# A hybrid recurrent block with product-key retrieval: one dense block searched from SBUF during the query, a place of its own for the first products' buffers, and staged weights in front

## The chip, the cores and the metric

The kernel runs on one core of one Trainium2 chip. The metric is the time of one execution on the device, in microseconds (us), taken several times; lower is better. The engines are TensorE (PE, with its weight loads shown as PEld), VectorE (DVE), ScalarE (ACT), GpSimd (POOL) and SyncE (SP), which here only issues transfers. Every engine works through its own queue in order.

## What is computed

One layer over 1024 tokens of width 1024, in float32. In the notation of the reference:

```python
xn = rms_norm(h, norm1_g)
p = xn @ w_in                                   # 1024 -> 1536: xa, gate, us (512 each)
ya = rg_lru_group(xa, gate, ...)                # conv of 4 taps, two sigmoid gates, a linear scan, times gelu(gate)
yb = s5_group(us, ...)                          # 32 groups, 64 complex states, chunked scan, gelu, GLU
h = h + concat[rms_norm(ya), rms_norm(yb)] @ w_out
x = rms_norm(h, norm2_g)
q = x @ wq                                      # 8 heads, two halves of 128 each
s1, s2 = q1 @ k1.T, q2 @ k2.T                   # 128 keys each
v1, i1 = top_k(s1, 16); v2, i2 = top_k(s2, 16)  # then the best 16 of the 256 sums v1 + v2
e = i1 * 128 + i2; g = softmax(best 16)         # 8 x 16 = 128 experts of 16384 per token
out = h + sum_e g * gelu(u_tab[e] . x) * v_tab[e]
result = rms_norm(out, normf_g)
```

## The kernel before, in words

**Order.** Most of the code is written as generators ("threads") that a small planner, `Merge`, interleaves: it keeps a modelled time for each engine and always continues the thread whose time plus bias is least. A thread that yields a name waits for that flag, one that yields a function waits until it is true. So the order in which instructions are traced is the planner's. A scheduler below it may move an instruction ahead on its engine where it thinks its inputs are there; `tc.keep_in_program_order(ins)` ties an instruction behind the one traced just before it on its engine. `begin` (L268) and the dense stage at the end stand under `manual_schedule`, in the order written. The planner's helper records every operation, so nearly all rows of the profile have its line, L146, and one goes by the names of tiles.

**Splits.** Matrix products run in float32r with each operand split into a high part (a ScalarE copy) and a low part (a VectorE subtraction), and three products for each pair.

**The front (`front`, L150).** `begin` loads, on SP, eight pieces of w_in (`w0`) and eight tiles of the transposed x (`xr`), and on POOL eight tiles of x (`xs`). For each of the eight it splits the weights (`wnext`, L230) and x (`split_x`), adds 24 products to eight accumulators (`held`) in PSUM, and takes some steps of the S5 set-up (`setup`, a generator on VectorE, as many steps as `PLAN` says). Then it makes four more weight pairs, tiles 8 to 11 of `wseq`, through the tag `wr` with two buffers, runs the set-up to its end, takes two squares for the first norm (`squares`, ScalarE), copies the accumulators to `Vt`, and puts the first two products of xa (`pj_product`) into PSUM. `rsqrt_x` (L210) makes the norm's factor and spreads it with products (`spr`) to `rstdb`; every projection after this is scaled by it. S5 (`quarter`), the RG-LRU (`lru_setup`, L682, and `lru`) and the remaining projections (`proj`) follow, interleaved; `wfill` keeps nine weight pairs ahead.

After that come the GLU, the two group norms (`norm`, L857) and the output product. `wo_half` (L841) loads eight tiles of w_out for a half (`wor`, two buffers), and splits each into `woh` and `wol`. `norm` makes for each of four tiles the scaled high part `ah`, the low part `al` and the square, and the sum of the squares at the end gives the factor `rg` with which the products `wop` are added to `h`. For group A these tiles are yA, in pools `fo` and `fa` that take over SBUF of the projections.

**The retrieval (`peer`, L1024).** Tokens are eight blocks of 128. Three blocks (5 to 7, "gather" blocks) fetch the chosen rows of the tables with indirect transfers on POOL (128 rows per token for u and for v, 768 row steps in all, each a transfer and one VectorE instruction). Five blocks (0 to 4, "dense" blocks) compute all experts: first products `ap` with the u table, its gelu to `aa` and to DRAM (`A_d`), then, weighted with a matrix G, products `vp` with the v table.

`query` (L1061) computes q and the scores, for the gather blocks first (`part` 0), then for the dense blocks (`part` 1): head by head, 5 blocks, each score tile copied by ScalarE to `sc` and, for dense blocks, stored to `S_d` in DRAM. During it run the top-k of the gather blocks (`topks`) and their first rows (`gathers`). `top16` (L1125) is five VectorE instructions: max of 8, index, replace, max, index.

After the query the pools `pkg` and `pq` are closed, and `ph1` (the buffers `aa` and later `hr`) and `pk2` are opened in their SBUF. `ahead` (L1500) makes the first products of 97 tiles, in half tiles; `steps` counts the halves. `choose` (L1248) searches the dense blocks one after another with `topk` (L1158), which loads the block's scores from `S_d` into `s`, runs 16 `top16` on them, and then goes on through the sums. The very first max of block 0 is pinned in program order. For block 0 each of the generator's yields waits until `steps` has reached `BEGIN + RATE * k`; later blocks are paced by `groups`. `build` (L1273) builds G with one-hot products `gp`; its group n waits for `steps >= LEAD + n` (LEAD is 23). Rows in between are limited by `allow`: 72 (`FIRST`) until step 23, then 1.6 more for each step. What is left of the rows is spread over the dense stage.

Of the kernel before, what the change touches and what calls it, by code (L numbers as in the profile page):

```python
# [149 lines left out]
def front(tc, a, cst, nd, mg):  # L150
# [79 lines left out]
    def wnext():  # L230

        parts = wseq[len(wmade)]
        if len(wmade) < 8:
            r = parts[0]
        else:
            r = pw.tile([P, 256], F32, tag="wr", name="wr", bufs=2)
            w = 256 // len(parts)
            for i, x in enumerate(parts):
                nc.sync.dma_start(r[:, w * i:w * i + w], x)
        h = pw.tile([P, 256], F32R, tag="wh", name="wh")  # L240
        lo = pw.tile([P, 256], F32R, tag="wl", name="wl")
        S.activation(h, r, AF.Copy)
        V.tensor_tensor(lo, r, h.bitcast(F32), ALU.subtract)
        wmade.append((h, lo))
# [20 lines left out]

    held = [(pu if s < 2 else pj if s < 4 else pt)("usp")[:, :256] for s in range(L)]

    def begin():  # L268
# [5 lines left out]
        for k in range(8):  # L274
# [3 lines left out]
            xrs.append(xr)  # L278
        for _ in range(WARM):
            PE.matmul(held[7][:, :P], ident, ident, start=True, stop=True)  # L280
        st, sq = setup(), squares()
        for k in range(8):
# [7 lines left out]
            xrs.append(xr)  # L290
            for _ in range(PLAN[k]):
                next(st)
            if k > 4:
                next(sq)
        for _ in range(4):
            wnext()
        for _ in st:
            pass
        for _ in range(2):
            next(sq)  # L300
# [4 lines left out]
        for i in range(2):  # L305
            pre[0, 0, i] = pp = pj("pj")
            pj_product(pp, wmade[8:12], i)
        for _ in sq:
            pass
# [372 lines left out]
    def lru_setup():  # L682
        tc.keep_in_program_order(S.dma_start(lamt, a["lru_lam"]))
        S.activation(e_, lamc, AF.Abs)
# [156 lines left out]
    def wo_half(half):  # L841

        for n in range(2):
            for k in range(4):
                if half:
                    yield "half0" if (n, k) >= (1, 2) else "cols0"
                r = po.tile([P, 512], F32, name="wor", tag="wor", bufs=2)
# [9 lines left out]
    def norm(grp, ys, dh, dl):  # L857

        gs, tot = pu("gs"), rstdb
        for k in range(4):  # L860
# [4 lines left out]
            yield  # L865
            sq = po.tile([P, T], F32, name="sq2", tag="sq2") if k else tot
# [151 lines left out]
PACE = 2.0  # L1018
WARM, PLAN = 8, (2, 6, 3, 3, 3, 3, 3, 1)
FIRST, STEP, KT, LEAD = 72, (1.6, 1.6), 2, 23  # L1020
BEGIN, RATE, FAST = 2, 0.68, 0.9


def peer(tc, a, cst, pools, h, nx, mg):  # L1024
# [36 lines left out]
    def query():  # L1061
# [13 lines left out]
        for part, (blocks, dh, dl) in enumerate(((gblocks, nx.xGh, nx.xGl), (dblocks, xDh, xDl))):  # L1075
# [6 lines left out]
            for h_ in range(8):  # L1082
# [23 lines left out]
                for n, b in enumerate(blocks):  # L1106
# [3 lines left out]
                    yield  # L1110
                    sc = pq.tile([P, 256], F32, tag="sc", name="sc", bufs=6)
# [7 lines left out]

    pkg = pools.open("pkg")  # L1120
# [28 lines left out]

    rows = pools.open("rows", "right", bufs=ROWS)  # L1150
# [6 lines left out]

    def topk(b):  # L1158
        if b >= ND:
            yield "found"  # L1160
            v, ix = found[b - ND]
        else:
# [6 lines left out]
            for h in range(8):  # L1169
                for f in range(2):  # L1170
                    top16(s[:, h, f], v[:, f, h], ix[:, f, h], b == dblocks[0] and f == 0)
# [368 lines left out]
    mg.run([(1.0, topks()), gr], until="q")  # L1540
    mg.run([], until="chosen")
    pools.close("pkg", "pq")
    ph1 = pools.open("ph1")
# [367 lines left out]
```

## Time and profile before

| | |
|---|---|
| median of 3 runs | 2580.09 us (2578.77 to 2582.99) |
| the profiled execution | 2573.88 us, its span 2572.1 us |
| busy, share of the span | PE 97%, PEld 88%, DVE 92%, ACT 52%, POOL 45% |
| instructions | 40777 |
| moved by DMA | 752.77 MB, mean 293 GB/s |

The stretches of the run, by what TensorE does in them: the front up to about 360 us, the query to about 590, first products and the building of G to about 1424, then the dense stage. In the page's 40 slices VectorE is at eight tenths or more in most slices, with dips around 270 to 350, near 1250 to 1420 and at the start.

In a row of a timeline stand start and length in us, engine, line, operation, output and inputs, shapes, and in brackets the idle time of the engine just before, with what ended it. In a row of stretches stand the stretch and its length, then busy time (and instructions) of PE, PEld, DVE, ACT and POOL, the granted clock of TensorE, the DMA share and GB/s. In the chain of waits stand start, length and what the run waited for.

### The profile page before, as it was taken

Reading aid. Unit: us, or ns where it says so; the run is one execution under the profiler, and the core shown is the slowest. Engines: PE = TensorE matmul, PEld = TensorE weight load, DVE = VectorE, ACT = ScalarE, POOL = GpSimd, SP = SyncE. Lnnn points to the kernel's source line nnn. Section 1 sums busy time; section 2 is a strip of 40 time slices with the busy share of each in tenths; the row PEclk is TensorE's granted clock in tenths of the full one; section 3 lists DMA queues with packets and bytes.
Section 4 is the critical chain, followed back from the end, with each engine's and each line's share of the span. In section 5 each row is a group of like instructions: output and inputs, shape, how many; then the busy total and the mean of one; then the engine's idle time right before and its main releaser. Section 6 shows DMA issues by size and latency. Waiting matters only on the chain.

```text
span 2572.1 us, 40777 instructions
## 1 busy us (share of the span) xinstructions
PE 2486.4 (97%) x14639; PEld 2252.0 (88%) x14639; DVE 2363.1 (92%) x4545; ACT 1332.5 (52%) x2389; POOL 1152.1 (45%) x803
## 2 busy tenths in 40 slices
PE   8998999999989999999999999999999999999997
PEld 7776889999989999999999988888888888888886
DVE  7998669997999999999977699999999999999998
ACT  5567434332468777877877444333344344333442
POOL 1000000353456466675554465555556556555551
PEclk9999999999999999999999999999999999999999
DMA  5113124687899999999999999999999999999994
GB/s 186 31 43 111 65 90 139 209 279 270 280 351 353 338 326 333 351 333 335 356 367 350 359 384 357 353 353 356 354 348 370 355 356 351 352 359 353 350 350 152
DMA packets 302201, 752.77 MB, mean 293 GB/s; under 512 B 29744, under 2 KB 128240, under 8 KB 297264
## 3 DMA queue, kind: packets, MB, share of 16 engines
q0 software_dynamic: 112896, 411.09, 43.9%
q1 hardware_dynamic: 186576, 336.28, 36.8%
q10 hardware_dynamic: 2528, 2.80, 0.3%
q8 instruction: 115, 1.88, 0.3%
q14 instruction: 86, 0.70, 0.1%
HBM read 662.92 MB, written 85.98 MB: 291 GB/s over the span
## 4 chain that ended last, share of the span: by engine, by line
PE 62%; DVE 27%; DMA 4%; issue 4%; ACT 2%; POOL 1%; SPq 0%; DVEq 0%; ACTq 0%; POOLq 0%
PE vp L146 26%; PE ap L146 17%; PE total L146 7%; DVE row L146 4%; PE qp L146 4%; DVE hb L146 3%; PE wop L146 3%; PE gp L146 2%; DVE ul L146 2%; DVE oh L146 2%; DVE ohA L146 2%; DVE ix L146 2%; DVE v L146 1%; PE pj L146 1%; DVE ohB L146 1%
## 5 line engine op out<-in xcount | busy, mean ns | idle before, releaser
L1339 POOL DMA_INDIRECT row<-in_peer_u_dram,idx x384 | 562.5, 1465 | 697.5 <-DVE act L146 268.3
L1339 POOL DMA_INDIRECT row<-in_peer_v_dram,idx x384 | 576.7, 1502 | 439.1 <-DVE hb L146 273.3
L146 PE MATMUL ap<-xDl,uh 128*128 128x320 f32 x2048 | 645.5, 315 | 9.0 <-ACT aa L146 8.2
L146 PE MATMUL ap<-xDh,ul 128*128 128x320 f32 x2048 | 635.6, 310 | 5.4 <-DVE ul L146 5.2
L146 PE MATMUL ap<-xDh,uh 128*128 128x320 f32 x2048 | 634.9, 310 | 0.0
L146 DVE SCALAR_TENSOR_TENSOR hb<-row,act,hb 128x1024 f32<-128x1024 f32 x384 | 494.0, 1286 | 6.7 <-DMA row<-in_peer_v_dram,idx 1.8
L146 DVE CUSTOM_DVE_ANT_0 row<-row,xg 128x1024 f32<-128x1024 f32 x384 | 458.7, 1219 | 3.0 <-DMA row<-in_peer_u_dram,idx 2.6
L146 PE MATMUL vp<-vl,hh 128*128 128x512 f32 x1024 | 398.7, 389 | 0.0
L146 PE MATMUL vp<-vh,hl 128*128 128x512 f32 x1024 | 398.5, 389 | 0.0
L146 PE MATMUL vp<-vh,hh 128*128 128x512 f32 x1024 | 398.5, 389 | 0.0
L146 PEld LDWEIGHTS ap<-xDl,uh 128*128 128x128 f32 x2048 | 386.1, 189 | 12.0 <-ACT aa L146 9.5
L146 PEld LDWEIGHTS ap<-xDh,ul 128*128 128x128 f32 x2048 | 386.2, 189 | 8.3 <-DVE ul L146 7.0
L146 PEld LDWEIGHTS ap<-xDh,uh 128*128 128x128 f32 x2048 | 385.7, 188 | 0.0
L146 ACT ACTIVATE gq<-gt 128x640 f32<-128x640 f32 x128 | 174.4, 1363 | 319.2 <-DVE hr L146 242.1
L146 PEld LDWEIGHTS vp<-vh,hh 128*128 128x128 f32 x1024 | 192.2, 188 | 40.2
L146 PEld LDWEIGHTS vp<-vl,hh 128*128 128x128 f32 x1024 | 192.2, 188 | 39.5 <-issue 0.4
L146 PEld LDWEIGHTS vp<-vh,hl 128*128 128x128 f32 x1024 | 192.2, 188 | 38.8
L146 ACT ACTIVATE ohB<-ohB,kt 128x128 f32<-128x128 f32 x480 | 202.2, 485 | 0.0
L146 PE MATMUL gp<-ohB,ohA 128*128 128x128 f32 x1280 | 172.1, 277 | 18.7 <-DVE ohB L146 14.8
L146 ACT ACTIVATE aa<-ap 128x320 f32<-128x320 f32 x194 | 84.1, 435 | 199.0 <-PE ap L146 183.2
L146 PEld LDWEIGHTS gp<-ohB,ohA 128*128 128x128 f32 x1280 | 158.9, 191 | 27.8 <-issue 11.5
L146 DVE TENSOR_TENSOR ul<-ur,uh 128x1024 fp32r<-128x1024 f32 x128 | 156.1, 1220 | 20.0 <-ACT uh L146 20.0
(450 smaller groups left out, 4457.6 us busy)
## 6 DMA issues: line engine op xcount, KB each, us to landing
ur<-in_uT_dram SPq DMA_DIRECT2D x128, 512.0 KB
vr<-in_peer_v_dram SPq DMA_DIRECT2D x128, 512.0 KB
gt<-G_d SPq DMA_DIRECT2D x32, 1280.0 KB
G_d<-gs SPq DMA_DIRECT2D x79, 512.0 KB
A_d<-aa SPq DMA_DIRECT2D x96, 320.0 KB
hr<-A_d SPq DMA_DIRECT2D x96, 320.0 KB
wqr<-in_wq_dram SPq DMA_DIRECT2D x31, 512.0 KB
row<-in_peer_u_dram,idx POOLq DMA_INDIRECT x384
```

The costliest lines, as they stand in the source:

```text
L146: return fn(*args, **kw)
L1339: G.indirect_dma_start(out=r, out_offset=None, in_=a["peer_v" if at >= P else "peer_u"], in_offset=bass.IndirectOffsetOnAxis(ap=idx[n][:, ...
```

## The change

In front, weight tiles 8 to 11 get places of their own (`wp`, in the pool `fx`), are loaded on SP right behind the transposed x, and are split inside the last of the eight steps, ahead of that step's set-up and square. The rest of the set-up and of the squares moves behind the first two products of xa, one square after each set-up step. The high parts of tiles 12 to 19 and the first instruction of `lru_setup` are pinned in program order. In `wo_half`, five of the eight tiles of half 0 (`OWN`) come through three buffers `wor0` in `fa` instead of `wor`. `norm` for group A makes all four high and low parts first, then the squares.

In the retrieval, ScalarE copies the scores of dense block 0 into one SBUF tile `s0` (8 heads x 2 x 128) and they are neither stored nor loaded again. A thread `search0` with bias 0.0 runs beside the query from the flag `split` on, which `query` sets when it has issued the last weight split: for each head whose copy has been traced (`seen`) it runs the two `top16`, the first max of each pinned. `topk` of block 0 takes these results, so 17 yields are left of it; `BEGIN` and `RATE` become 1 and 1.0. `ph1` is opened on the right side, before the pool of the rows, instead of on the left after `pkg` and `pq` are closed.

```diff
@@ wnext
         if len(wmade) < 8:
             r = parts[0]
+        elif len(wmade) < 12:
+            r = wp[:, len(wmade) - 8]
         else:
             r = pw.tile([P, 256], F32, tag="wr", name="wr", bufs=2)
...
-        S.activation(h, r, AF.Copy)
+        ins = S.activation(h, r, AF.Copy)
+        if 12 <= len(wmade) < 20:
+            tc.keep_in_program_order(ins)
         V.tensor_tensor(lo, r, h.bitcast(F32), ALU.subtract)
...
+    wp = px.tile([P, 4, 256], F32, name="wp")
@@ begin
+        for n in range(4):
+            for i, x in enumerate(wseq[8 + n]):
+                nc.sync.dma_start(wp[:, n, P * i:P * i + P], x)
         for _ in range(WARM):
             PE.matmul(held[7][:, :P], ident, ident, start=True, stop=True)
...
             xrs.append(xr)
+            if k == 7:
+                for _ in range(4):
+                    wnext()
             for _ in range(PLAN[k]):
                 next(st)
             if k > 4:
                 next(sq)
-        for _ in range(4):
-            wnext()
-        for _ in st:
-            pass
-        for _ in range(2):
-            next(sq)
         Vt[0] = pvt.tile([P, 16, L, 16], F32, name="Vt", tag="Vt", bufs=2)
...
             pj_product(pp, wmade[8:12], i)
+        for _ in st:
+            next(sq, None)
         for _ in sq:
             pass
@@ lru_setup
-        S.activation(e_, lamc, AF.Abs)
+        tc.keep_in_program_order(S.activation(e_, lamc, AF.Abs))
@@ wo_half
-                r = po.tile([P, 512], F32, name="wor", tag="wor", bufs=2)
+                own = half == 0 and (n, k) in OWN
+                r = pa_.tile([P, 512], F32, name="wor0", tag="wor0", bufs=3) if own else \
+                    po.tile([P, 512], F32, name="wor", tag="wor", bufs=2)
@@ norm
-        for k in range(4):
+
+        def parts(k):
             g_ = cols[:, k, 7 + grp:8 + grp]
             S.activation(dh[:, k], ys[k], AF.Copy, scale=g_)
             yield
             V.scalar_tensor_tensor(dl[:, k], ys[k], g_, dh[:, k].bitcast(F32), ALU.mult, ALU.subtract)
             yield
+        if grp == 0:
+            for k in range(4):
+                yield from parts(k)
+        for k in range(4):
+            if grp:
+                yield from parts(k)
             sq = po.tile([P, T], F32, name="sq2", tag="sq2") if k else tot
@@ constants
+OWN = ((0, 0), (0, 2), (1, 0), (1, 1), (1, 3))
-BEGIN, RATE, FAST = 2, 0.68, 0.9
+BEGIN, RATE, FAST = 1, 1.0, 0.9
@@ query
+                    if part and n == 0:
+                        if h_ == 0:
+                            s0.append(pk.tile([P, 8, 2, P], F32, name="s", tag="s", bufs=1))
+                        S.activation(s0[0][:, h_], p_[:, :256].rearrange("p (f k) -> p f k", f=2), AF.Copy)
+                        seen[0] += 1
+                        yield
+                        continue
                     sc = pq.tile([P, 256], F32, tag="sc", name="sc", bufs=6)
@@ peer
+    s0, seen = [], [0]
...
+    ph1 = pools.open("ph1", "right")
     rows = pools.open("rows", "right", bufs=ROWS)
...
+    def search0():
+        yield "split"
+        v = pk.tile([P, 2, 8, 16], F32, name="v", tag="v")
+        ix = pk.tile([P, 2, 8, 16], U32, name="ix", tag="ix")
+        for h in range(8):
+            yield lambda: seen[0] > h
+            for f in range(2):
+                top16(s0[0][:, h, f], v[:, f, h], ix[:, f, h], f == 0)
+        s0.append((v, ix))
+        mg.flag("s0")
+        yield
...
+        elif b == dblocks[0]:
+            v, ix = s0.pop()
         else:
             s = pk.tile([P, 8, 2, P], F32, name="s", tag="s", bufs=1)
...
-                    top16(s[:, h, f], v[:, f, h], ix[:, f, h], b == dblocks[0] and f == 0)
+                    top16(s[:, h, f], v[:, f, h], ix[:, f, h])
...
-    mg.run([(1.0, topks()), gr], until="q")
+    mg.run([(1.0, topks()), (0.0, search0()), gr], until="q")
     mg.run([], until="chosen")
+    mg.run([], until="s0")
     pools.close("pkg", "pq")
-    ph1 = pools.open("ph1")
     pk2 = pools.open("pk2", bufs=2)
```

## The prediction

> **What bounds the kernel now.** I read the page first, then the stretches, and only then the instructions on either side of each hole in TensorE's work.
>
> ```profile
> PE 2486.4 (97%) x14639; PEld 2252.0 (88%) x14639; DVE 2363.1 (92%) x4545; ACT 1332.5 (52%) x2389; POOL 1152.1 (45%) x803
> ```
>
> ```profile
> 30.00:60.00 30.00, 20.54 (x115) 16.44 (x115) 21.29 (x83) 17.19 (x39) 3.43 (x12) 0.83 0.16 45
> 150.00:200.00 50.00, 46.95 (x274) 36.17 (x273) 49.69 (x81) 33.83 (x45) 0.00 (x0) 0.97 0.18 42
> 590.00:600.00 10.00, 8.78 (x61) 8.33 (x59) 0.00 (x0) 1.56 (x5) 2.14 (x3) 1.00 0.97 354
> 700.00:720.00 20.00, 17.38 (x120) 16.79 (x120) 20.00 (x72) 11.09 (x27) 10.87 (x9) 1.00 0.93 320
> 720.00:740.00 20.00, 16.29 (x107) 14.67 (x106) 20.00 (x66) 10.42 (x27) 9.87 (x8) 1.00 0.93 307
> 740.00:760.00 20.00, 17.40 (x119) 16.43 (x120) 20.00 (x63) 13.51 (x36) 12.01 (x9) 1.00 1.03 408
> 850.00:900.00 50.00, 47.36 (x335) 46.01 (x335) 50.00 (x172) 34.38 (x85) 22.83 (x16) 1.00 0.94 334
> 1000.00:1050.00 50.00, 45.37 (x323) 44.32 (x323) 50.00 (x167) 33.65 (x84) 21.62 (x16) 1.00 0.94 335
> 1600.00:1800.00 200.00, 200.00 (x985) 172.80 (x984) 194.67 (x179) 78.08 (x86) 107.33 (x80) 1.00 0.96 355
> ```
>
> The columns after the length are busy time of PE, PEld, DVE, ACT and POOL, then clock, DMA share and GB/s. TensorE sets the time: the dense stage (1600 to 1800) has no hole. So an edit pays only where it closes a hole, or where the engine ahead of a hole is freed. All holes together are 2572.1 - 2486.4 = 85.7 us. In the front (150 to 200) VectorE is fuller than TensorE, so time that only TensorE wins there does not all reach the end. From 700 to 760 TensorE misses 2.62 + 3.71 + 2.60 = 8.9 us with VectorE at 100%.
>
> **Edit 1, own weight places (the w_in tiles 8 to 11).** TensorE, then ScalarE, then VectorE, around the first hole:
>
> ```profile
> 29.91 1.12 PE L146 MATMUL usp<-wh,xl 128*128 128x256 f32 x8
> 40.49 0.80 PE L146 MATMUL pj<-xl,wh 128*128 128x512 f32 x1 [9.46 <-ACT Vt L146]
> 41.08 0.63 PE L146 MATMUL pj<-xh,wl 128*128 128x512 f32 x1
> 41.51 0.63 PE L146 MATMUL pj<-xh,wh 128*128 128x512 f32 x1
> ...
> 44.66 0.39 PE L146 MATMUL pj<-xh,wh 128*128 128x512 f32 x1
> 44.88 0.39 PE L146 MATMUL pj<-xl,wh 128*128 128x512 f32 x1
> ```
>
> ```profile
> 30.73 0.42 ACT L146 ACTIVATE wh<-wr 128x256 fp32r<-128x256 f32 x1 [2.03 <-DMA wr<-in_w_in_dram]
> ...
> 40.07 2.27 ACT L146 ACTIVATE Vt<-usp 128x256 f32<-128x256 f32 x8
> ```
>
> ```profile
> 37.05 0.42 DVE L146 TENSOR_TENSOR wl<-wr,wh 128x256 fp32r<-128x256 f32 x1 [2.69 <-ACT wh L146]
> 38.12 0.42 DVE L146 TENSOR_TENSOR wl<-wr,wh 128x256 fp32r<-128x256 f32 x1 [0.64 <-ACT wh L146]
> ...
> 45.48 1.00 DVE L146 TENSOR_SCALAR sq<-rc 128x8 f32<-128x8 f32 x1 [4.28 <-ACT xs L146]
> ```
>
> The held products end at 31.03. The third weight tile has to wait for a buffer, is split on ScalarE just ahead of the wl at 37.05, and the accumulators' copies (Vt) stand behind it on ScalarE, so TensorE starts 9.46 us late. With places of their own the four tiles are all issued right behind the last xT transfer on SP: eight issues of 64 KB each, with nothing behind them on SP that is needed sooner. The second tile landed at 30.7 when two were asked for; I take 32 for the fourth. Then come its split (0.42), one Square (about 1.2, like the 128x1024 ah at 255.04 below, 1.13) and the first Vt copy, so TensorE restarts near 33.9 (32 + 0.42 + 1.2 + 0.3): 6.6 us sooner. VectorE's holes are 2.69 + 0.64 + 4.28 = 7.6 us; it will still wait about 3 us for the same tiles, but the eight Vt copies then end near 36 and the five squares left near 42, 3.5 us ahead of 45.48, so it wins about 4.5. The pins on the later splits, and on the Abs of the RG-LRU setup, only keep them behind the square root and the broadcast; the products that need those weights wait for that broadcast anyway, and if that cover failed four splits of 0.42 would show. Both engines are nearly full later in the front, so the term lies between the two: **-5.5** (ends -3, if only part of VectorE's hole goes, and -8, if tiles land by 30).
>
> A hole also costs clock. Products start 0.43 us apart after the hole (41.08, 41.51) and 0.22 apart later (44.66, 44.88). A shorter hole shows up too:
>
> ```profile
> 78.12 2.08 PE L146 MATMUL gt<-xc,wab 128*128 128x512 f32 x2 [2.28 <-ACT r__1031 L146]
> ```
>
> ```profile
> 78.00:80.00 2.00, 1.88 (x3) 0.85 (x4) 1.90 (x4) 0.37 (x2) 0.00 (x0) 0.50 0.00 0
> ```
>
> After 2.28 us of idling the clock was 0.50, so my remaining hole of 2.9 us keeps its slow start and I book no clock gain in this term. The Trainium skill ("TensorE: Matmul & The Clock Gate", Part 1) has the clock fall only after an idle window of about 3.4 us; by that the slow start would go too, an estimate of 1.7 us more if it costs what it does at the seam below. The row at 78 us disagrees, and it decides.
>
> **Edit 2, staged w_out tiles and the order in norm.**
>
> ```profile
> 252.30 0.63 ACT L146 ACTIVATE woh<-wor 128x512 fp32r<-128x512 f32 x1 [2.79 <-DMA wor<-in_w_out_dram]
> 254.51 0.63 ACT L146 ACTIVATE woh<-wor 128x512 fp32r<-128x512 f32 x1 [1.58 <-DMA wor<-in_w_out_dram]
> 255.04 1.13 ACT L146 ACTIVATE ah<-yA,cols 128x1024 fp32r<-128x1024 f32 x1
> ```
>
> ```profile
> 256.23 0.80 PE L146 MATMUL wop<-wol,ah 128*128 128x512 f32 x1 [4.33 <-ACT ah L146]
> ```
>
> ```profile
> 256.23 5.92 PE wop L146 x13
> ```
>
> Two buffers make the third and fourth tile late, and the third scaled input (ah) stands behind them on ScalarE. With five places all four tiles of the first column half are asked for at once, and all ah and al are made ahead of the squares. The hole is 4.33. The chain of waits (second fence) has the 13 products after it at 5.92 us, where 13 at the spacing of 0.22 take 2.9, so 3.0 more are lost to the clock. The squares move back by at most three ah of 1.13, but are no longer behind 4.4 us of waiting, so the norm that releases the PSUM tiles is not later. I keep 2.3 of the 7.3 for transfers that share the DMA engines with the loads of x: **-5** (ends 0, if ScalarE then waits for the first four instead, and -7.3).
>
> **Edit 3, the seam after the query.** ScalarE, TensorE and VectorE there, and TensorE's clock:
>
> ```profile
> 601.68 1.28 ACT L146 ACT_TABLE_LOAD   x1 [9.10 <-DMA S_d<-sc]
> ```
>
> ```profile
> 603.46 0.53 PE L146 MATMUL ap<-xDl,uh 128*128 128x320 f32 x1 [4.68 <-ACT aa L146]
> ```
>
> ```profile
> 603.79 0.49 DVE L146 MAX8 v<-s 128x8 f32<-128x128 f32 x2 [15.56 <-DMA s<-S_d]
> ...
> 605.88 1.21 DVE L146 CUSTOM_DVE_ANT_0 row<-row,xg 128x1024 f32<-128x1024 f32 x1
> ```
>
> ```profile
> 603.00:605.00 2.00, 1.54 (x6) 1.54 (x7) 1.21 (x9) 1.68 (x3) 0.00 (x0) 0.65 0.21 83
> 605.00:607.00 2.00, 2.00 (x10) 2.00 (x9) 2.00 (x8) 0.00 (x0) 0.00 (x0) 0.50 0.21 81
> ```
>
> The first product buffer (aa) lies where score tiles lay whose stores were still out, so ScalarE waited 9.10 us and TensorE 4.68; the clock then lost 2 x 0.35 + 2 x 0.50 = 1.7. With ph1 at a place of its own on the right side both go: **-6.4** (ends -5, where the 1.28 us table load shows, and -6.4). Eight stores of 128 KB and one load of 1 MB leave SP's queue; its work lies beside, so that is 0. The eight copies to s0 take the place of eight of the same size: 0.
>
> VectorE sat 15.56 us in front of the pinned first search. 603.79 to 605.88 holds one head short of one index, so a head costs about 2.3 us, eight heads 18. When they run is set by the flag that `search0` waits for, set once the last q weights are split:
>
> ```profile
> 574.72 1.22 DVE L146 TENSOR_TENSOR wql<-wqr,wqh 128x1024 fp32r<-128x1024 f32 x1
> ```
>
> So no split of the query is behind them: seven heads fill 576 to 592, the eighth follows its scores. What they push back is some nine gather rows of 1.21 us, which fit into the 15.56 that VectorE regains. The searches are pinned; behind them on VectorE stand rows and the splits of the second u tiles, not needed for a while. **0** (ends 0, and +3, if one split comes a head's search late).
>
> After the seam VectorE has 18 us less to do and starts 15 us sooner, and BEGIN and RATE spread block 0's remaining 17 steps up to step 18, ahead of the build at 23. The 8.9 us missing from 700 to 760 should fall to what later blocks lose at the same point (50 - 47.36 = 2.6 and 50 - 45.37 = 4.6, mean 3.6). That is -5.3; I take **-4** since block 1's search now cannot start early (ends 0 and -12, if the next block's start gains too).
>
> **Sum.** -5.5 - 5 - 6.4 + 0 - 4 = -20.9 us. The profiled execution took 2573.88 (span 2572.1 and 1.8 around it), so 2553.0; the median of the runs, 2580.09, lies 6.2 above the profiled one, so about **2559.2**. All good ends give -33.7, all bad ends -5.
>
> **Rivals.** *Only the seam counts.* VectorE stays the pace of the front and the staged tiles only move the wait: -3, 0, -6.4, +1 and 0 make -8.4, 2571.7 of the median. For it: 49.69 of 50 at 150 to 200. Against it: VectorE's own holes at 37 to 45 go as well. *The edits do not do what they say in time:* the holes close, but from 600 to 1250 VectorE, full in every row above, returns them as later waits for ohB and ul; only about -3 is left, 2577. Against it: it has 18 us less to do there. *The other side: pinned splits parked on ScalarE.* The eight pinned high parts (tiles 12 to 19) still go through two buffers, and where one is not there, all of ScalarE waits, with S5 and the RG-LRU behind it, instead of passing it by.
>
> ```profile
> 36.61 0.42 ACT L146 ACTIVATE wh<-wr 128x256 fp32r<-128x256 f32 x1 [5.46 <-DMA wr<-in_w_in_dram]
> ```
>
> At this row's 5.46 a tile, less what the first two tiles save since they can be loaded far ahead, six waits make 32.8 us against -20.9: +11.9, 2592. It decides from 20.9 / 6 = 3.5 us a tile. Against it: by the time of the pins VectorE, which frees the buffers, is no longer held up by its own hole of 4.28.
>
> **How the numbers follow.** The forecast 0.62, only the seam 0.22, nothing left 0.10, parked splits 0.06. A measurement of this kernel tells about 0.2%, 5.2 us, from no change: the first two are faster, with some of the second's lower part falling within; the third is no change. So faster 0.83, same 0.11, slower 0.06. The likeliest case alone spans 2549 to 2569. Down to 2546 takes in half of the good ends, up to 2577 the second rival and part of the third, and about 2 in 10 is left out.
>
> **What would show it.** Right: the hole ahead of the first pj product under 4 us and its start near 33.9; no wait for wor between two ah; the first aa without a wait for S_d, and no 15 us on a MAX8; PE over 18.5 of 20 in the three stretches after the build's start. Wrong: ScalarE waits for wr between 40 and 80 us that are longer than before; a TensorE wait for ul right after the seam; a hole at the first wop product that only changes its releaser to the squares or the norm; or a first ap product after the seam (603.46) that comes less than 10 us sooner although the holes ahead of it are gone.

## The result, and the profile after

The changed kernel took 2556.0 us (median of 6 runs, 2552.3 to 2556.9), the kernel before, measured beside it, 2579.5 us (2578.0 to 2583.0). The ratio is 0.9908 with a 95% interval of 0.9895 to 0.9922. Measured a second time (below) it was 0.9921, 0.9894 to 0.9947. The forecast was 2559.2 us, the range 2546 to 2577. The profiled execution took 2555.21 us with a span of 2553.3 us, against 2573.88 and 2572.1 before: 18.7 us less in the profiles, 23.5 us less in the medians. Where the other 5 us are is one of the questions below.

From the page of the changed kernel, the busy time of the engines over the span:

```profile
PE 2482.5 (97%) x14639; PEld 2252.1 (88%) x14639; DVE 2364.9 (93%) x4545; ACT 1337.2 (52%) x2389; POOL 1157.9 (45%) x803
```

TensorE's busy time fell by 3.9 us only, its holes from 85.7 to 2553.3 - 2482.5 = 70.8 us. The stretches of the changed kernel that answer to those shown of before (length, busy time of PE, PEld, DVE, ACT and POOL, clock, DMA share, GB/s):

```profile
30.00:60.00 30.00, 26.13 (x168) 20.59 (x168) 27.93 (x96) 19.43 (x43) 3.41 (x12) 0.94 0.11 29
150.00:200.00 50.00, 45.53 (x275) 35.33 (x273) 49.82 (x79) 33.43 (x44) 0.00 (x0) 1.00 0.18 41
590.00:600.00 10.00, 10.00 (x70) 10.00 (x69) 10.00 (x36) 2.16 (x5) 7.71 (x6) 1.00 0.95 361
700.00:720.00 20.00, 19.93 (x144) 19.50 (x143) 20.00 (x41) 14.86 (x37) 16.95 (x11) 1.00 1.03 370
720.00:740.00 20.00, 18.28 (x127) 17.36 (x127) 18.44 (x45) 13.89 (x34) 16.05 (x13) 1.00 1.04 409
740.00:760.00 20.00, 18.77 (x135) 18.35 (x134) 18.88 (x59) 14.42 (x32) 9.39 (x8) 1.00 1.04 408
850.00:900.00 50.00, 48.11 (x344) 47.17 (x344) 50.00 (x146) 39.77 (x93) 25.78 (x17) 1.00 0.95 337
```

Against before, VectorE does 6.6 us more between 30 and 60 us (27.93 for 21.29), the seam (590 to 600) has no hole and a full VectorE, and from 700 to 760 us TensorE misses 3.0 us where it missed 8.9.

The first pj product in the changed kernel, on TensorE:

```profile
33.46 0.51 PE L146 MATMUL pj<-xl,wh 128*128 128x512 f32 x1 [2.29 <-ACT Vt L146]
33.80 0.60 PE L146 MATMUL pj<-xh,wl 128*128 128x512 f32 x1
34.19 0.63 PE L146 MATMUL pj<-xh,wh 128*128 128x512 f32 x1
```

The hole of 9.46 us is 2.29 us, and the start, 33.46, is 7.0 us sooner. In this execution the products behind it still start 0.34 to 0.43 us apart.

ScalarE and then TensorE ahead of the gs products:

```profile
244.36 1.14 ACT L146 ACTIVATE ah<-yA,cols 128x1024 fp32r<-128x1024 f32 x1
245.40 0.62 ACT L146 ACTIVATE woh<-wor 128x512 fp32r<-128x512 f32 x1
245.92 1.14 ACT L146 ACTIVATE ah<-yA,cols 128x1024 fp32r<-128x1024 f32 x1
247.11 0.63 ACT L146 ACTIVATE woh<-wor 128x512 fp32r<-128x512 f32 x1
247.65 0.67 ACT L146 ACTIVATE sg<-glp,cols 128x512 f32<-128x512 f32 x1
248.22 1.15 ACT L146 ACTIVATE ah<-yA,cols 128x1024 fp32r<-128x1024 f32 x1
```

```profile
248.62 0.39 PE L146 MATMUL wop<-wol,ah 128*128 128x512 f32 x1
...
260.01 1.95 PE L146 MATMUL gs<-ones,rstdb 128*128 128x1 f32 x16 [1.14 <-DVE rstdb L146]
```

No ah waits for a wor tile, and the hole of 4.33 us behind the first wop products is gone. What is left is 1.14 us ahead of gs.

ScalarE at the seam:

```profile
585.91 0.39 ACT L146 ACTIVATE sc<-sp 128x256 f32<-128x256 f32 x1 [0.35 <-PE sp L146]
586.32 1.28 ACT L146 ACT_TABLE_LOAD   x1
589.10 0.44 ACT L146 ACTIVATE aa<-ap 128x320 f32<-128x320 f32 x1 [1.50 <-PE ap L146]
```

The table load follows the last score copy without the wait of 9.10 us, and the first aa copy waits for its own product.

To see where time is won, the start times of six events cut each trace into stages (us, each a difference of two start times in the trace). "Front" ends with the first wop product; the others with the first gs product, the first ap product, the third copy of aa, the 49th copy of aa, and the first vp product. All rows but the last two are single profiled executions; the two kernels with added products (below) are not in the table.

| kernel | front | to gs | to first ap | to 3rd aa | to 49th aa | to first vp |
|---|---|---|---|---|---|---|
| before | 250.2 | 16.1 | 323.6 | 19.0 | 202.7 | 664.3 |
| before, again | 255.0 | 14.5 | 323.1 | 19.1 | 204.0 | 665.5 |
| before, third | 254.4 | 14.6 | 323.6 | 18.6 | 203.7 | 675.4 |
| changed | 248.6 | 11.4 | 323.7 | 12.5 | 196.9 | 663.5 |
| changed, again | 247.9 | 11.3 | 326.0 | 12.5 | 198.0 | 661.5 |
| front undone | 254.6 | 11.8 | 325.7 | 12.5 | 197.4 | 662.5 |
| staged tiles undone | 248.5 | 15.8 | 323.9 | 12.5 | 200.1 | 667.0 |
| ph1's place undone | 250.9 | 11.2 | 328.4 | 12.8 | 196.8 | 661.0 |
| pace undone | 249.1 | 11.1 | 323.3 | 12.5 | 199.7 | 663.1 |
| search behind the query, pace undone | 250.5 | 11.5 | 323.8 | 17.5 | 204.4 | 663.6 |
| search released after the query | 252.0 | 11.2 | 323.8 | 16.4 | 197.8 | 663.4 |
| pins undone | 248.4 | 11.2 | 323.3 | 12.5 | 196.0 | 661.6 |
| median with the stage as before | 254.5 | 15.2 | 323.6 | 19.0 | 203.7 | 665.5 |
| median with the stage as changed | 249.1 | 11.3 | 323.9 | 12.5 | 197.4 | 662.5 |

The last two rows take, for each stage, the runs in which that stage's edit is undone or done: for the front the three of before and "front undone" against all others but "pins undone"; to gs the three of before and "staged tiles undone" against the rest; the other stages the three of before against the runs of the changed kernel that keep the search in the query ("pins undone" among them), "ph1's place undone" left out at the 3rd aa. The differences are -5.4, -3.9, +0.3, -6.5, -6.3 and -3.0, together -24.8; the medians of the runs differ by 23.5 and, measured a second time, by 22.1. So the 18.7 us between the two first profiles are the exception, and most of it lies in the front: its -1.5 there is -5.4 between medians. The last stage of the third profile of before is 10 us longer than the others', which is not explained.

### The profile page after: what moved, and what is told of

Its sections match the earlier page's. It is cut to its first block, busy times and chain, and to the rows that moved or that the text cites. A ratio compares the mean times of both kernels' runs of the same rounds, so it can differ in the third digit from the quotient of the medians.

```text
span 2553.3 us, 40753 instructions
## 1 busy us (share of the span) xinstructions
PE 2482.5 (97%) x14639; PEld 2252.1 (88%) x14639; DVE 2364.9 (93%) x4545; ACT 1337.2 (52%) x2389; POOL 1157.9 (45%) x803
## 3 DMA queue, kind: packets, MB, share of 16 engines
q0 software_dynamic: 112896, 411.09, 43.9%
## 4 chain that ended last, share of the span: by engine, by line
PE 60%; DVE 28%; issue 5%; DMA 4%; ACT 2%; POOL 1%; DVEq 0%; SPq 0%; POOLq 0%; ACTq 0%
PE vp L146 26%; PE ap L146 17%; PE total L146 6%; DVE hb L146 5%; DVE row L146 3%; PE wop L146 3%; PE qp L146 3%; DVE ul L146 2%; PE gp L146 2%; DVE oh L146 2%; DVE ohA L146 2%; DMA ur<-in_uT_dram 1%; DVE ix L146 1%; DVE ci L146 1%; DVE v L146 1%
## 5 line engine op out<-in xcount | busy, mean ns | idle before, releaser
L1379 POOL DMA_INDIRECT row<-in_peer_u_dram,idx x384 | 581.5, 1514 | 664.7 <-DVE scv L146 242.1
L1379 POOL DMA_INDIRECT row<-in_peer_v_dram,idx x384 | 563.4, 1467 | 448.8 <-DVE hb L146 262.7
L146 DVE TENSOR_TENSOR h<-h,vp 128x1024 f32<-128x1024 f32 x128 | 155.6, 1216 | 19.6 <-PE vp L146 18.2
```

The lines of the kernel that those rows point to most:

```text
L146: return fn(*args, **kw)
L1379: G.indirect_dma_start(out=r, out_offset=None, in_=a["peer_v" if at >= P else "peer_u"], in_offset=bass.IndirectOffsetOnAxis(ap=idx[n][:, ...
```

## The experiments

**The front undone.** The four own weight places, their early splits, the pins and the new order of set-up and squares go; everything else stays.

```diff
-        elif len(wmade) < 12:
-            r = wp[:, len(wmade) - 8]
...
-        ins = S.activation(h, r, AF.Copy)
-        if 12 <= len(wmade) < 20:
-            tc.keep_in_program_order(ins)
+        S.activation(h, r, AF.Copy)
```

> Edit 1 undone (no own weight places, no pins on ScalarE), the rest as in the changed kernel. Theory, from the two traces: the first pj product goes back from 33.5 to 40.5 us, but VectorE and a slow clock near 82 to 88 us had taken nearly all of that back, so that by 186 us only 1.4 us are lost, and so the whole takes about 1.4 us more than the changed kernel: about 2557.5 us against 2556. Rival, the term as predicted: 5.5 us are lost by 186 us and at the end, about 2561.5 us.

Measured: 2562.1 us beside 2582.5 for before, ratio 0.9922 (0.9905 to 0.9938). The front took 254.6 us, 5.9 more than in the profiled change and 4.4 more than in the profile of before, though up to the first wop product its TensorE program is that of before. The run times cannot tell 1.4 from 5.5 us. That holds for the four kernels measured together here (the front, the staged tiles, ph1's place and the pace undone): their ratios of 0.9922 to 0.9933 lie inside the 0.9894 to 0.9947 that the unedited change showed the second time, so what each edit is worth is read from single traces. In the trace the loss is 5.9 us at the first wop product and 8 to 9 us from the first ap product on. So the theory was built on a profile of before that was not typical (next experiment), and the rival, the predicted 5.5, holds.

**The kernel before, twice more.** Nothing edited.

> The kernel before once more, nothing edited, for a second profile of it. Theory: its stretch of clock 0.50 behind the held sums stays (a hole of 9.5 us), the one near 78 us comes at another time or a second one follows near 87 us, and the first wop product lies up to 4.4 us behind the 250.15 us of its first profile. Rival: the stretch belongs to the program, 250.15 within 0.5 us.

> As the run before it: a third profile of the unchanged kernel before. Theory: the first wop product between 250 and 255 us, with the clock's stretch near 80 or near 90 us, and later as the stretch covers more of the 40 products that stand there without a hole. Rival: 250.15 us within 0.5 us.

Measured: first wop products at 254.96 and 254.41 us. Stretches of the first profile of before:

```profile
78.00:82.00 4.00, 3.88 (x8) 2.07 (x8) 3.79 (x7) 2.14 (x5) 0.00 (x0) 0.58 0.00 0
86.00:97.00 11.00, 10.78 (x93) 9.75 (x94) 11.00 (x17) 6.93 (x11) 0.00 (x0) 1.00 0.18 50
```

and of the second:

```profile
78.00:82.00 4.00, 2.70 (x8) 1.20 (x8) 3.79 (x7) 3.09 (x6) 0.00 (x0) 1.00 0.00 0
86.00:97.00 11.00, 10.77 (x55) 8.77 (x56) 10.41 (x17) 4.72 (x9) 0.00 (x0) 0.54 0.17 50
```

The same program has its slow clock once at 78 to 82 us, where TensorE has few products, and once at 86 to 97 us, where it works almost without a hole: 93 matmuls were done in those 11 us in the first execution and 55 in the second. Three of four executions of this front had the late one. The profile on which the prediction stood was the exception, 4.3 us short of the median of 254.5. The theory held.

These two profiles differ from the first at the seam as well. TensorE and ScalarE in the second:

```profile
596.63 1.22 PE L146 MATMUL sp<-kT,qt 128*128 128x128 f32 x4 [3.64 <-issue]
```

```profile
604.68 1.28 ACT L146 ACT_TABLE_LOAD   x1 [3.74 <-PE ap L146]
```

The two waits from which Edit 3 was made up, 9.10 us of ScalarE for the stores and 4.68 us of TensorE for aa, stand in neither. The table load waits for TensorE's own products (3.74 us here, 4.11 in the third profile), and TensorE loses its time among the last scores (3.64 + 0.27 us here, 1.90 + 1.39 in the third). The stage is as long all the same: 19.1 and 18.6 us against 19.0.

**The changed kernel again.**

> The changed kernel once more, nothing edited. Theory: where the clock of 0.50 falls between 70 and 96 us differs from one execution to the next of the same program (78 to 82 us in the profiled run of before, 86 to 97 us in the run with edit 1 undone, whose program is that of before up to there), so that the first wop product (248.6 us in the profiled run of the change) moves by up to 3 us with no edit at all. Rival: the stretch belongs to the program, and the first wop product comes within 0.5 us of 248.6.

Measured: 2556.7 us beside 2578.8, ratio 0.9921 (0.9894 to 0.9947). Stretches of the first profile of the change, then of this one:

```profile
72.00:80.00 8.00, 4.79 (x16) 2.26 (x16) 7.83 (x14) 5.91 (x9) 0.00 (x0) 1.00 0.09 26
82.00:90.00 8.00, 7.97 (x46) 6.38 (x47) 7.73 (x12) 3.50 (x6) 0.00 (x0) 0.60 0.24 68
```

```profile
72.00:80.00 8.00, 6.90 (x20) 3.31 (x18) 7.83 (x14) 6.00 (x9) 0.00 (x0) 0.57 0.11 33
82.00:90.00 8.00, 8.00 (x48) 6.64 (x47) 8.00 (x12) 3.38 (x6) 0.00 (x0) 0.57 0.19 51
```

The clock differs at 72 to 80 us, with the same program. Behind the hole of 2.29 us at 33 us it was 0.50 for some 3.5 us in the first profile and 1.00 here (0.94 and 1.00 as the mean of 30 to 60 us). The first wop product moved by only 0.7 us, but over the seven profiles that share this front it lies between 247.9 and 252.0. The theory held.

**Products that keep TensorE busy.** 26 products with a zero matrix, which add nothing to the sum, in the holes of 77 to 82 us; then 36 more, most of them at 31 and 70 us.

```diff
                     us_product(o, s + e, k, w)
+                    if s + e == 0 and k in (3, 4):
+                        for _ in range(6 if k == 3 else 20):
+                            nc.tensor.matmul(o, zero, w[k][1], start=False, stop=False)
```

> The changed kernel with 26 added products of 128x256 with a zero matrix, which add zero to the first usp sum, laid into TensorE's short holes between 77 and 82 us. Theory: they keep TensorE's clock at 1.00 through 82 to 90 us, the 41 products there take 4.3 us instead of 6.7, and the first wop product comes 2 us or more sooner than in the unedited change of the same call. Rival: VectorE is the pace there, the clock or not, and the first wop product comes within 0.5 us of it or later.

> As the kernel before it, with 18 more such products behind the held sums (31 to 33 us) and 16 more in the hole of 2.3 us at 70 to 72 us. Theory: the first pj products also start at 0.22 us instead of 0.43 us apart, 1.5 to 2 us more are won by 40 us, and no stretch of clock 0.50 is left between 30 and 100 us; the first wop product comes 3 to 5 us sooner than in the unedited change. Rival: VectorE and ScalarE set the time of the next holes, so that it wins no more than the kernel before it.

Measured: 2555.8 us (ratio 0.9908, 0.9883 to 0.9932) and 2562.4 us (0.9940, 0.9918 to 0.9961), with 2556.7 for the unedited change beside them. In the first of them:

```profile
82.00:90.00 8.00, 8.00 (x72) 7.02 (x71) 8.00 (x14) 5.10 (x8) 0.00 (x0) 1.00 0.25 68
```

```profile
247.97 0.39 PE L146 MATMUL wop<-wol,ah 128*128 128x512 f32 x1
```

The clock held at 1.00 through 82 to 90 us, and 72 matmuls were done there instead of 46 to 48, some ten of them the added ones. But the first wop product came as in the unedited kernel (247.94). So the rival has the number; its reason, that VectorE is the pace with the clock or without it, the trace does not bear out. Two rows of VectorE lie ahead of and behind the stretch, the first two `Wr<-inr,Ec` after 60 us. In the change again, then with the 26 products:

```profile
69.62 0.68 DVE L146 TENSOR_TENSOR Wr<-inr,Ec 128x508 f32<-128x508 f32 x1
113.70 0.69 DVE L146 TENSOR_TENSOR Wr<-inr,Ec 128x508 f32<-128x508 f32 x1 [2.56 <-PE inr L146]
```

```profile
71.19 0.68 DVE L146 TENSOR_TENSOR Wr<-inr,Ec 128x508 f32<-128x508 f32 x1
112.61 0.69 DVE L146 TENSOR_TENSOR Wr<-inr,Ec 128x508 f32<-128x508 f32 x1 [1.88 <-PE inr L146]
```

At the second row VectorE waits for TensorE. In each of the two fronts the time between the two rows grows as the mean clock falls:

| kernel | mean clock, 82 to 98 us | first row | second row | between |
|---|---|---|---|---|
| before | 1.00 | 76.21 | 115.70 | 39.5 |
| before, again | 0.68 | 76.71 | 120.64 | 43.9 |
| before, third | 0.68 | 76.19 | 120.18 | 44.0 |
| front undone | 0.68 | 76.47 | 120.31 | 43.8 |
| 26 products added | 1.00 | 71.19 | 112.61 | 41.4 |
| changed | 0.80 | 70.56 | 114.34 | 43.8 |
| changed, again | 0.79 | 69.62 | 113.70 | 44.1 |
| ph1's place undone | 0.68 | 71.12 | 116.55 | 45.4 |
| search released after the query | 0.59 | 70.70 | 117.38 | 46.7 |

The other three profiles with the new front and its pins fit in (0.79, 0.79 and 0.68 with 44.0, 44.1 and 45.6 us). From the second row to the first wop product it is 134.2 to 134.6 us in all of these, and 135.4 with the 26 products. So the held clock was worth some 2.5 us at the second row. About 1 us of that went later: at 148 us ScalarE waits 5.10 us for a w_in load, where it waits 4.14 in the change again. The rest is hidden, since this execution was 0.6 to 1.6 us late at the first row already, after a slower clock between 34 and 42 us (0.65, against 0.80 and 1.00 in the two profiles of the change). That the first wop products agree is thus a coincidence of one profile; the run times are too coarse for 1.5 us. With the further products the clock is 1.00 as well, but the planner put a gt product 5.3 us later, the time between the rows was 43.3 us, and the front took 251.9 us; whether a better place for them would win something was not tried.

**The pins alone undone**, those on the eight weight splits; the one on Abs stays.

```diff
-        ins = S.activation(h, r, AF.Copy)
-        if 12 <= len(wmade) < 20:
-            tc.keep_in_program_order(ins)
+        S.activation(h, r, AF.Copy)
```

> Only the pins of the eight weight splits (tiles 12 to 19) on ScalarE undone; own weight places, staged tiles, seam and search as in the changed kernel. Theory: the pins cost and save nothing; the first wop product lies between 247.9 and 250.9 us as in the profiles of the change, about 2556 us. Rival: the pins keep VectorE's wl late (ScalarE waits for wr of 1.55, 1.02 and 1.23 us between 80 and 86 us); without them these waits go and the first wop product comes 2 us or more sooner than 247.9.

Measured: 2559.3 us (2551.7 to 2565.9) beside 2581.0, ratio 0.9919 (0.9897 to 0.9941). TensorE's first pj product, and the stretch of it:

```profile
38.19 0.80 PE L146 MATMUL pj<-xl,wh 128*128 128x512 f32 x1 [6.58 <-ACT Vt L146]
```

```profile
30.00:60.00 30.00, 23.23 (x145) 19.33 (x143) 27.72 (x110) 19.30 (x43) 3.84 (x12) 0.89 0.15 44
```

Without the pins four more splits and the RG-LRU's first steps stand ahead of the Vt copies, and TensorE restarts 4.7 us later than in the change. Yet the first wop product came at 248.4. VectorE did 27.72 us of work between 30 and 60 us here, as in the change (27.93), and 21.48 us in the kernel with the front undone. So, as far as one profile can show it, what counts is that the own places close VectorE's holes, and TensorE's restart carries little: the first `Wr<-inr,Ec` row came at 71.92 us here, against 69.62 to 71.12 in the seven profiles with pins.

**The staged tiles undone.**

```diff
-                own = half == 0 and (n, k) in OWN
+                own = False
...
-            for k in range(4):
-                yield from parts(k)
         for k in range(4):
-            if grp:
-                yield from parts(k)
+            yield from parts(k)
```

> Edit 2 undone (w_out through two buffers, the scaled inputs and squares in the old order), the rest as in the changed kernel. Theory: TensorE's hole of about 4.3 us ahead of the first wop product comes back, the gs product comes 4.8 us later than in the changed kernel, and the loss stays to the end: about 2561 us. Rival: the front and the search make up for it later, less than 2 us more at 583 us (the first ap product) and at the end: 2556 to 2558 us.

Measured: 2563.3 us beside 2582.5, ratio 0.9929 (0.9903 to 0.9956). TensorE has the hole again:

```profile
254.68 0.80 PE L146 MATMUL wop<-wol,ah 128*128 128x512 f32 x1 [4.41 <-ACT ah L146]
```

The gs products came 4.4 us later than in the change and the first ap product 4.6 us later: the loss stays, as the theory had it.

**The place of the first products' buffers undone.** ph1 is opened on the left again, behind the closing of the score tiles; the search stays in the query.

```diff
-    ph1 = pools.open("ph1", "right")
...
     pools.close("pkg", "pq")
+    ph1 = pools.open("ph1")
```

> Only the place of the first products' buffers undone: they are again opened where the score tiles lay, while block 0's scores are still searched from SBUF. Theory: the wait of about 9 us on ScalarE and of 4 to 5 us on TensorE at the seam (about 590 to 600 us) comes back, the clock is slow for some 4 us behind it, and 6.5 us are lost at the third product; the 9 us gained after the seam, from VectorE, stay: about 2562.5 us at the end. Rival: VectorE uses the hole for rows and index work and gives 3 us or more of it back by 760 us, so that only 0 to 3.5 us more are left at the end.

Measured: 2561.5 us beside 2582.5, ratio 0.9926 (0.9909 to 0.9944). ScalarE at its seam, and two stretches:

```profile
597.68 1.28 ACT L146 ACT_TABLE_LOAD   x1 [4.57 <-DMA S_d<-sc]
598.97 0.89 ACT L146 ACTIVATE aa<-ap 128x320 f32<-128x320 f32 x2
```

```profile
570.00:590.00 20.00, 20.00 (x142) 19.66 (x140) 20.00 (x108) 4.62 (x12) 5.69 (x6) 1.00 0.66 223
590.00:600.00 10.00, 9.93 (x70) 9.45 (x69) 10.00 (x44) 4.51 (x10) 4.61 (x4) 1.00 0.79 225
```

ScalarE waits 4.57 us for the stores, half of before, and TensorE misses 0.07 us. From the first ap product to the third aa copy it took 12.8 us, 0.3 more than in the change and 6.2 less than before. The theory fell: with the search in the query, the place closes next to nothing. Between the first gs and the first ap product it lost 4.5 us against the median; its loads of u and wq stand in another order on SP there. But the clock's mean was also 0.96 in each of 400 to 440, 480 to 520 and 520 to 560 us, where the first profile of the change has 1.00; the change again has 0.96 in the last two of them and lost 2.3 us in this stage with nothing edited. So these 4.5 us cannot be put down to the edit.

**The search put back behind the query**, with its scores read back and the old pace; the buffers keep their own place.

```diff
-                    if part and n == 0:
...
-        elif b == dblocks[0]:
-            v, ix = s0.pop()
...
-BEGIN, RATE, FAST = 1, 1.0, 0.9
+BEGIN, RATE, FAST = 2, 0.68, 0.9
...
-    mg.run([(1.0, topks()), (0.0, search0()), gr], until="q")
+    mg.run([(1.0, topks()), gr], until="q")
```

> Block 0's search put back behind the query, from scores read back into SBUF, with the old pace constants; the first products' buffers stay at their own place. Theory: the seam stays closed on TensorE (first ap product near 583.7, the third aa copy near 596), VectorE waits for the scores again and has 18 us more to do after it, and the 9 to 10 us gained between 690 and 760 us go: aa copies 48 to 180 come 9 us later than in the changed kernel, about 2565 us in all. Rival: VectorE was not the cause of that gain, the leads change by 3 us or less, about 2557 to 2559 us.

Measured: 2574.6 us beside 2578.8, ratio 0.9979 (0.9965 to 0.9993): most of the gain is gone. TensorE and VectorE at the seam:

```profile
586.42 0.71 PE L146 MATMUL sp<-kT,qt 128*128 128x128 f32 x4 [0.24 <-issue]
587.90 0.71 PE L146 MATMUL sp<-kT,qt 128*128 128x128 f32 x4 [0.77 <-issue]
...
590.75 0.71 PE L146 MATMUL sp<-kT,qt 128*128 128x128 f32 x4 [1.98 <-ACT sc L146]
```

```profile
599.95 0.49 DVE L146 MAX8 v<-s 128x8 f32<-128x128 f32 x2 [15.49 <-DMA s<-S_d]
```

```profile
570.00:590.00 20.00, 17.75 (x122) 16.81 (x120) 11.52 (x19) 4.04 (x11) 15.32 (x13) 1.00 0.96 342
590.00:600.00 10.00, 9.25 (x53) 9.25 (x54) 0.05 (x1) 2.99 (x6) 0.00 (x0) 0.83 0.79 308
```

The own place did not keep the seam closed: TensorE loses 3.0 us on the last scores, as it does in the second and third profile of before, then the clock is 0.83, and the stage takes 17.5 us. After the seam 7.5 us more go (204.4 against 196.9). In all the first vp product came 14.8 us later than in the change, 1.9 of them from the front, and the medians differ by 17.9, where the theory had 9.

**The search released after the query**, its scores still in SBUF, without store or load.

```diff
     def search0():
-        yield "split"
+        yield "q"
```

> Block 0's scores still stay in SBUF (no store, no load of them), but their search is released only when the whole query is done, not during it. Theory: the seam stays closed on TensorE, because one of five score stores of each head is gone and the first buffers have their own place (third aa copy within 1 us of the first ap product's lead, near 596 to 598); VectorE no longer waits 15 us, but its 18 us of search fall behind the seam, and 5 to 8 us of the gain between 690 and 800 us go: about 2562 us. Rival: what counts is only that the scores need not be read back; then all but 2 us of the gain stays, 2556 to 2558 us.

Measured: 2563.1 us beside 2581.0, ratio 0.9924 (0.9902 to 0.9946). TensorE, and the stretches:

```profile
588.72 0.71 PE L146 MATMUL sp<-kT,qt 128*128 128x128 f32 x4 [1.34 <-issue]
590.20 1.22 PE L146 MATMUL sp<-kT,qt 128*128 128x128 f32 x4 [0.77 <-issue]
...
611.31 0.63 PE L146 MATMUL ap<-xDh,ul 128*128 128x320 f32 x1 [3.55 <-DVE ul L146]
```

```profile
570.00:590.00 20.00, 18.10 (x126) 17.33 (x125) 16.48 (x63) 5.13 (x13) 16.64 (x12) 1.00 0.88 295
590.00:600.00 10.00, 9.80 (x58) 9.80 (x59) 10.00 (x59) 3.20 (x7) 1.08 (x3) 0.83 0.74 252
```

On VectorE the search runs from 582 to 604 us here, where it runs from 564 to 589 in the change: the last score copy starts at 592.63, so some 11 us of it lie behind the query. VectorE's wait of 15 us is gone, one of five stores is gone, the place is own, and still the stage to the third aa takes 16.4 us. Then ul comes 3.55 us late, behind the search and the steps that follow it. The lag behind the change grows from 7.2 us at the third aa copy to 14.5 at the fifth, and 6.5 us of it are won back before the 49th, so that the stage after the seam is as in the change (197.8). Both the theory (seam closed) and its rival (2 us) fell.

What goes with the seam is in the row of 570 to 590 us. In the change it reads:

```profile
570.00:590.00 20.00, 20.00 (x141) 19.79 (x140) 20.00 (x110) 5.77 (x12) 3.75 (x4) 1.00 0.56 173
```

With the search there, VectorE is full of it and takes few gathered rows: POOL is busy for 3.75 us and the DMA share is 0.56 (5.69 and 0.66 with ph1's place undone). Without it POOL has 15 to 17 us of gathers and the share is 0.96 and 0.88. Over all profiles of this study, nine have a share of 0.56 to 0.75 there and take 12.5 to 12.8 us to the third aa; five (before three times, and the two above) have 0.88 to 0.96 and take 16.4 to 19.1, whatever the place of the buffers. That the stores come out late because they share the DMA engines with gathers fits all of these. But ahead of the last scores the traces name only "issue" or ScalarE's own copy, not the stores, and no run slowed the gathers alone; so it is argued, not shown.

**The pace alone undone**, BEGIN and RATE as before.

```diff
-BEGIN, RATE, FAST = 1, 1.0, 0.9
+BEGIN, RATE, FAST = 2, 0.68, 0.9
```

> Only the two pace constants undone (BEGIN 2 and RATE 0.68 instead of 1 and 1.0). Theory: the 9 us gained between 690 and 760 us come from VectorE having 18 us less to do after the seam, whatever the pace; the lead at 760 us changes by 2 us or less and the whole stays within 2 us of the changed kernel's 2556. Rival: the spreading of block 0's steps closes the holes; with the old pace the missing busy time of 8.9 us in 700 to 760 comes back, about 2565 us.

Measured: 2563.1 us (2557.0 to 2567.5) beside 2582.5, ratio 0.9933 (0.9916 to 0.9950). In the profile the stage after the seam is 199.7 us, 2.3 above the median of the change and within its spread of 196.0 to 200.1. The rival's 9 us are excluded by the trace. Whether the pace is worth 0 or 2 us is not settled, and the time of the runs would allow more.

No kernel of these beats the changed one by more than its measurement can tell.

## Why the prediction was right, and where not

**Edit 1, -5.5.** Measured -5.4 between the medians of four and seven profiles, front against front, and 5.9 with the edit undone. The restart was forecast at 33.9 and came at 33.46. The gain is there early: at the first `Wr<-inr,Ec` row it is 5.8 us between the medians, and 5.7 between the two first profiles. Two parts of the reasoning did not hold. "The term lies between the two" engines: the run without pins speaks for VectorE's share alone. And the pins do not "only keep them behind the square root": they hold the hole at 2.29 us instead of 6.58, at no price at the end. The clock's stretch at 82 to 97 us was not in the sum at all, since the one profile at hand showed it elsewhere. It costs both fronts: they mostly take 44 us from the first row to the second, where 39.5 and 41.4 were enough at a clock of 1.00. That it drops out of the difference was luck, for the prediction does not weigh it.

"I book no clock gain" was right in the first profile and wrong in the second, where the clock stayed at 1.00 behind the same hole and VectorE's first row came 0.9 us sooner. The Trainium skill ("TensorE: Matmul & The Clock Gate", Part 1) says that the activity window runs free of the kernel, so that the same program meets it in another phase in each execution. The stretches of two executions of before and of two of the change agree with that. Its idle window of about 3.4 us does not stand as a bound for the hole: 2.29 us were enough in one execution and not in the other.

**Edit 2, -5.** Measured -3.9 between medians, and 4.4 with the edit undone. In the first profile it was -4.7, from 16.1 to 11.4; the other two of before took only 14.5 and 14.6. No wait for wor stands between two ah. Of the 7.3 us in sight 3.4 were not won, where 2.3 were kept back for shared transfers; no run tells what holds them.

**Edit 3, the seam, -6.4.** The size is right to 0.1 us (19.0 to 12.5), the step that gives it is not, so the agreement is luck. The prediction put it down to the place of ph1 and booked the search in the query at 0 there. With the place undone 0.3 us are lost; with the search undone and the place kept, 5.0. And the wait for the stores that the place was to remove stands in one of the three profiles of before only. What failed is the sentence that moves "some nine gather rows" into VectorE's regained time as if only VectorE's time were moved: each row is also a gather, and in every profile where these gathers fill the DMA engines from 570 to 590 us the seam is open.

**The search in the query, 0 (0 to +3).** Measured +0.3 between medians, with a spread of 323.3 to 328.4 us where before had 323.1 to 323.6; a split that comes late, as the end of +3 had it, cannot be told from the spread. The two kernels with added products took 326.9 and 326.3 us; with them the median of nine is 2.1 us above before, so the term may not be 0. The search was forecast at 576 to 592 us and ran from 564 to 589.

**After the seam, -4 (0 to -12).** Measured -6.3 up to the 49th aa copy and -3.0 from there to the first vp, the latter no larger than the spread between executions. This term was mis-sized. The reason given, 18 us less for VectorE, is not borne out: the kernel that releases the search late has some 11 us of it behind the query, loses for a while, and still takes 197.8 us for the stage. Its scores need no reading back; those of the kernel with the search undone do, VectorE starts on them at 600 us with the old pace, and it takes 204.4. Which of the two, the late start or the pace, costs most there was not told apart. The three stretches of 700 to 760 us were forecast at over 18.5 us of TensorE each and show 19.93, 18.28 and 18.77.

**The sum and the offset.** -20.9 was made against the profile of before and 6.2 added for the median. Of these 6.2 us, 4.3 are that profile's clock stretch in a place where it costs little. With the medians of the stages the sum is -24.8, and 2579.5 - 24.8 = 2554.7, where 2556.0 was timed. The forecast came out 3.2 us above the measured time, with terms that were 3.9 us too small in sum.

**The rivals.** "Only the seam counts" is out, since the front and the staged tiles each cost 4 us or more when undone. "The edits do not do what they say in time" is out: undone staged tiles still cost 4.6 us at the first ap product. "Pinned splits parked on ScalarE": the waits for wr behind the pins were 1.55, 1.02 and 1.23 us, under the 3.5 from which that case decides, and taking the pins away won nothing.

## What to carry to other kernels

Take a second profile of the kernel before, before the sum is made against it: here one stage differed by 4 us between executions of one program, as much as most terms of the sum, and the wait that one term was to close stood in one profile of three. When work on one engine is moved, ask also which transfers it thereby delays or lets start, and look at the DMA share of the stretch that it leaves and of the one that it enters. An edit that removes a wait for a buffer should be tried without its neighbours, for the wait may have been a late store and not the place.

## What the runs showed of the hardware

TensorE's granted clock falls to 0.50 at different times in executions of one program: at 78 to 82 or at 86 to 97 us in before, and behind a hole of 2.29 us in one execution of the change and not in another. Ahead of 100 us the stretch lasted from some 3 us (before) to some 13 us (search released after the query), and fewer matmuls were done while it lasted (93 against 55 in 11 us). Small products added in the holes of 77 to 82 us, which are 0.6 to 1.3 us long in the first profile of the change, held the clock at 1.00 from 82 to 98 us in both profiles taken.
